# Sums over keys in an attention kernel: four TensorE transposes per block replaced by VectorE's 32x32 transposes and one small TensorE transpose

## The chip, the cores and the metric

The kernel runs on one core of a Trainium2 chip. A core has five engines with instruction streams of their own, each executed in order: TensorE (PE in the profile, its weight loads PEld), VectorE (DVE), ScalarE (ACT), GpSimd (POOL) and SyncE (SP, which here only issues DMAs). They share SBUF (128 partitions) and synchronise by semaphores. TensorE writes its results to PSUM, whose banks hold 128 partitions of 512 float32 numbers. The metric is the device time of one execution in microseconds (us); lower is better.

## The reference, cut to what matters

The whole computation is one encoder layer over 2048 tokens: an input projection, a gated linear attention with 4 heads (group A), a latent attention with 4 heads (group B), an output projection and a layer norm. The change touches only the softmax of group B:

```python
def attend(blk):
    qn, qr = blk
    s = (jnp.einsum('bqhd,bkhd->bhqk', qn, k_nope, preferred_element_type=jnp.float32)
         + jnp.einsum('bqhr,bkr->bhqk', qr, k_r, preferred_element_type=jnp.float32))
    p = jax.nn.softmax(s, axis=-1)
    return jnp.einsum('bhqk,bkhv->bqhv', p.astype(v.dtype), v)
```

For each head and query, the exponentials of the scores less their maximum are summed over all 2048 keys, and the weighted values are divided by that sum. The kernel leaves the division to the output projection: it stores the reciprocal of the sum for every head and query, and multiplies by it there.

## The kernel before, in words

After the input projection and group A, the function `attention` works through 16 blocks. A block is one head and 512 queries (`QB`); four heads for one range of queries follow each other. Within a block the keys lie on the partitions: `scores(i, j)` computes the scores of a pair of key tiles, 2 x 128 keys against 512 queries, as 10 matmuls of 128x512 into one of two PSUM tiles `pS`, and there are 8 such steps j in a block. Float32 products are made of three matmuls of rounded parts (`mm3`), so each product has a high and a low operand (`ph` and `pl` for the exponentials).

What follows for each step: ScalarE copies the scores to an SBUF tile `s` (`copy`, L1571). VectorE folds them from PSUM into a running maximum `rm` of 128 partitions x 512 queries (`smax`, L1584; L1581 for step 0). After step 7 PE transposes `rm` (`tmax`, L1590), VectorE takes the maximum over the keys that are left (`rmax`, L1595), and PE spreads it over the partitions again into `mb` (`bmax`, L1602). VectorE subtracts it (`sub`, L1608), ScalarE takes the exponential (`exp`, L1612) and the high part (`phi`, L358), GpSimd the low part (`plo`, L364), and PE multiplies with the values into the PSUM tile `o` (`pv`, 6 matmuls a step, L412 to L414). A `pS` tile can be written again when `copy` and `smax` have read it.

Sums over keys: VectorE adds the exponentials of steps 0, 1, 2 and 5 into a PSUM tile `ap` (`acc`, L1635), GpSimd those of the other four into an SBUF tile of 128 x 2 x 512 named `acc` (L1638, L1640). `tot` (L1658, L1659) adds the two, so that `acc[:, 0]` holds, for each partition, a sum over 16 keys for each of the 512 queries. The 128 partitions are still to be added. `tsum` (L1671) transposes this 128x512 by four PE transposes of 128x128 into the PSUM tile `sx`, with the data as weights and the identity as the moving operand. `rcp` adds along the row on VectorE (L1677, a reduction of 128x512 to 128x4) and takes the reciprocal (L1678). `keep` (L1683) sends the 128x4 result to `r_s` in HBM from ScalarE's DMA queue, in pieces of 4 bytes, since neighbouring queries lie on neighbouring partitions.

The result in `o` is split into `ofh` (ScalarE, `oh`) and `ofl` (VectorE, `ol`), which both read the one PSUM bank of `o`, and multiplied with the value weights (`y`, `yc`). `sx`, the transposed maxima and `y` use the same bank in turn (`pX`, tag x). The output projection (`OutProj.load`) reads `r_s` back, broadcast over the partitions.

The order of the work is written out by hand: `PLACE` gives each piece a place in steps from the start of its own step (or, for the pieces once a block, from its step 7), `put` collects them, and they are traced in order of place; `in_order` ties each engine's instructions to this order. In these units a block is 8 steps. `tot` at 7 + 11.2 stands at 2.2 of the block two later, `tsum` at 3.04, `rcp` at 4.55, `keep` at 5.21. Around them stand, in that same later block: `smax` of step 1 at 2.21, the fourth `sub` of the block before at 2.37, scores of step 3 at 3 and of step 4 at 4, and the first `pv` of the block before at 4.35.

The last two blocks differ: their sums are stored as rows, by a PE transpose (`turn`, L1689) and a DMA from SyncE's queue (`rows`, L1696), and part of their work is placed among the output projection.

Of the kernel before, what the change touches and what calls it, by code (L numbers as in the profile page):

```python
# [9 lines left out]
F32 = mybir.dt.float32  # L10
# [3 lines left out]
ALU = mybir.AluOpType  # L14
AX = mybir.AxisListType
# [3 lines left out]
P = 128  # L19
# [10 lines left out]
QB = 512  # L30
# [62 lines left out]
    rmax=1.27,  # L93
    bmax=1.48,
    tot=11.2,
    tsum=12.04,
    rcp=13.55,
    keep=14.21,
    oh=12.34,
    ol=12.99,  # L100
    y=16.55,
    yc=16.9,
# [244 lines left out]
class K:  # L347
# [1190 lines left out]
    def attention(self):  # L1538
        tc, nc = self.tc, self.nc
        mm = nc.tensor.matmul  # L1540
        V, G, Ac = nc.vector, nc.gpsimd, nc.scalar
        NP = NKT // 2
        with ExitStack() as ctx:
# [3 lines left out]
            bs = ctx.enter_context(tc.tile_pool(name="bs", bufs=2, reuse_waits="tile"))  # L1547
            bank = lambda n, bufs=1: ctx.enter_context(tc.tile_pool(name=n, bufs=bufs, space=PSUM, reuse_waits="tile"))
            pM, pO, pX, pA, pS = bank("pM"), bank("pO"), bank("pX"), bank("pA"), bank("pS", 2)
            blocks = [(h, b) for b in range(NQB) for h in range(H)]  # L1550
            nb = len(blocks)
            stt = [dict(s=[None] * NP) for _ in blocks]
# [108 lines left out]
            def close(i, shape, name, other):  # L1661


                p, tag = other if i == nb - 1 else (pX, "x")
                return p.tile(shape, F32, tag=tag, name=name)

            def tsum(i):
                d = stt[i]
                d["x"] = close(i, [P, 4, P], f"sx{i}", (pA, "ap"))
                for e in range(4):  # L1670
                    nc.tensor.transpose(d["x"][:, e], d["as"][:, 0, e * P:(e + 1) * P], self.ident)  # L1671

            def rcp(i):

                d = stt[i]
                rc = bs.tile([P, 4], F32, tag="rc", name=f"rc{i}")
                V.tensor_reduce(rc, d["x"], AX.X, ALU.add)  # L1677
                V.reciprocal(rc, rc)  # L1678
                d["rc"] = rc

            def keep(i):
                h, b = blocks[i]
                Ac.dma_start(self.r_s[b][:, h].rearrange("o (e p) -> p (o e)", p=P), stt[i]["rc"])  # L1683

            def turn(i):

# [48 lines left out]
            def put(place, fn, *a):  # L1735
                todo.append((place, len(todo), fn, a))
# [5 lines left out]
            put(0.5, nc.sync.dma_start, wv, self.ins["wv"])  # L1742
            put(8.6, wv_hi)
            put(9.9, self.lo, wv_l, wv, wv_h, "pool")
            own = (("tot", tot), ("tsum", tsum), ("rcp", rcp), ("keep", keep), ("oh", oh), ("ol", ol), ("y", y), ("yc", yc))
            own_late = tuple(e for e in own if e[1] is not keep)
            for i in range(nb):
                for j in range(NP):
                    t = NP * i + j
# [80 lines left out]
            for c in range(4, NCH):  # L1830
                with fixed():
                    split(c + 2)
                    load(c + 4)
                    if 4 < c < NCH - 1:
                        op.load_res(rest[c + 1])
                    op.product(rest[c])
                    op.finish(rest[c])
                with self.after(*last.values()), fixed():
                    for f in {4: (tot, oh, ol), 5: (tsum, rcp), 7: (turn, y, rows, yc)}.get(c, ()):
                        f(nb - 1)  # L1840
                    if c == 6:
                        turn(nb - 2)
                        rows(nb - 2)
# [216 lines left out]
```

## Time and profile before

| | us |
|---|---|
| median of 3 runs | 1270.41 |
| lowest and highest | 1268.89, 1271.71 |
| the profiled execution | 1270.53 |
| its span in the profile | 1268.4 |
| first group of L1671 in the trace, block 0 | 643.6 |
| L1671 of block 13 | 1048.4 |
| last group of L1671, block 15 | 1147.9 |

The span runs from the first to the last recorded instruction; all times of views count from its start. A row of a group gives line, engine, operation, the tiles written and read, shapes and count, then busy time, mean duration in ns, and the engine's idle time before these instructions with what ended most of it. A row of the timeline gives start and duration in us, engine, line, operation, tiles and count; a bracket at its end gives idle time before it and what released it. Neighbouring instructions of a group stand in one row. PE's matmuls are pipelined, so their records overlap. "PEclk" is the clock granted to TensorE, in tenths of full speed in the page and as a fraction in the table of windows.

### The profile page before, as it was taken

The page shows a single profiled execution, that of the slowest core. Times are in us where ns is not written, and L with a number is a line of the kernel's source. Part 1 is how long each engine was busy: PE and PEld are TensorE (multiplying, and loading weights), DVE is VectorE, ACT ScalarE, POOL GpSimd, SP SyncE. Part 2 cuts the span into 40 slices and gives each one's busy share as a digit, 9 for nine tenths or more (in the row PEclk, how much of TensorE's full clock was granted, in tenths as well). Part 3 has the DMA queues.
Part 4 walks back from the last instruction along what each step waited for, and adds up shares of the span by engine and source line. Part 5 has one row for each costly group of instructions (what it writes and reads, how often), then busy time and mean ns, then how long its engine had stood idle before and what let it go on. Part 6 is the DMA issues. An engine that isn't in the chain of part 4 may idle for free.

```text
span 1268.4 us, 19649 instructions
## 1 busy us (share of the span) xinstructions
PE 1247.2 (98%) x6950; PEld 1100.2 (87%) x6950; DVE 893.5 (70%) x1610; ACT 727.9 (57%) x1177; POOL 718.6 (57%) x443
## 2 busy tenths in 40 slices
PE   8999999999999999989999999999999999999997
PEld 7999999999899999988788888888888888887886
DVE  6635555553665545564888888888888888389997
ACT  7544343454665444444888888888888888411110
POOL 0132323223265554430798888889999999935541
PEclk9999999999999999999999999999999999999999
DMA  8224555565857766747211111202133120376662
GB/s 297 76 82 124 136 144 137 144 134 159 274 173 211 210 187 204 211 133 199 76 32 53 40 45 42 59 9 59 58 92 92 42 42 26 122 231 195 208 191 100
DMA packets 188546, 160.10 MB, mean 126 GB/s; under 512 B 97206, under 2 KB 139838, under 8 KB 188448
## 3 DMA queue, kind: packets, MB, share of 16 engines
q1 hardware_dynamic: 180384, 156.72, 43.2%
q0 software_dynamic: 672, 2.10, 0.4%
q8 instruction: 55, 0.90, 0.3%
q10 hardware_dynamic: 7392, 0.03, 0.3%
q14 instruction: 43, 0.35, 0.1%
HBM read 102.79 MB, written 56.00 MB: 125 GB/s over the span
## 4 chain that ended last, share of the span: by engine, by line
PE 87%; issue 3%; DMA 3%; POOL 2%; DVE 2%; ACT 2%; SPq 1%; DVEq 0%; POOLq 0%; ACTq 0%
PE pz L1244 7%; PE ipm L1315 5%; PE o L412 5%; PE o L413 5%; PE o L414 4%; PE pS L1562 4%; PE pS L1563 4%; PE pS L1564 4%; PE pS L1565 4%; PE pS L1566 4%; PE ipa L412 4%; PE ipa L414 4%; PE ipa L413 4%; PE ipg L414 2%; PE ipg L413 2%
## 5 line engine op out<-in xcount | busy, mean ns | idle before, releaser
L364 POOL TENSOR_TENSOR pl<-s,ph 128x1024 fp32r<-128x1024 f32 x128 | 306.7, 2415 | 51.5 <-ACT ph L358 48.0
L1584 DVE TENSOR_TENSOR rm<-pS,rm 128x512 f32<-128x512 f32 x210 | 144.8, 690 | 36.3 <-ACT s L1571 30.7
L1571 ACT ACTIVATE s<-pS 128x1024 f32<-128x1024 f32 x128 | 131.2, 1025 | 61.3 <-PE pS L1566 51.7
L1608 DVE TENSOR_TENSOR s<-s,mb 128x1024 f32<-128x1024 f32 x128 | 151.2, 1213 | 8.9 <-PE mb L1602 8.2
L358 ACT ACTIVATE ph<-s 128x1024 fp32r<-128x1024 f32 x128 | 135.0, 1056 | 17.2 <-PE o L414 16.5
L1612 ACT ACTIVATE s<-s 128x1024 f32<-128x1024 f32 x128 | 131.4, 1049 | 9.4 <-DVE s L1608 9.3
L412 PE MATMUL ipa<-wah,xah 128*128 128x384 f32 (+1 forms) x384 | 128.8, 335 | 5.5 <-ACT wah L358 5.5
L413 PE MATMUL ipa<-wal,xah 128*128 128x384 f32 (+1 forms) x384 | 124.5, 324 | 0.0
L414 PE MATMUL ipa<-wah,xal 128*128 128x384 f32 (+1 forms) x384 | 124.5, 324 | 0.0
L1079 POOL TENSOR_TENSOR Sb<-Sb,Us 64x512 f32<-64x512 f32 x15 | 19.9, 1324 | 169.7 <-DVE Us L1071 160.6
L1562 PE MATMUL pS<-qh,ckvT_h 128*128 128x512 f32 x256 | 102.6, 401 | 0.8 <-DVE rm L1584 0.4
L412 PE MATMUL o<-ph,vh 128*128 128x512 f32 x256 | 101.1, 395 | 0.0
L1563 PE MATMUL pS<-ql,ckvT_h 128*128 128x512 f32 x256 | 100.0, 391 | 0.0
L1564 PE MATMUL pS<-qh,ckvT_l 128*128 128x512 f32 x256 | 99.9, 390 | 0.0
L1565 PE MATMUL pS<-rh,krs 128*128 128x512 f32 x256 | 99.9, 390 | 0.0
L1566 PE MATMUL pS<-rl,krs 128*128 128x512 f32 x256 | 99.8, 390 | 0.0
L414 PE MATMUL o<-ph,vl 128*128 128x512 f32 x256 | 99.8, 390 | 0.0
L413 PE MATMUL o<-pl,vh 128*128 128x512 f32 x256 | 99.7, 389 | 0.0
L1635 DVE TENSOR_TENSOR ap<-ap,s 128x512 f32<-128x512 f32 x120 | 83.0, 692 | 2.7 <-ACT s L1612 0.7
L412 PEld LDWEIGHTS ipa<-wah,xah 128*128 128x128 f32 x384 | 73.1, 190 | 8.4 <-ACT wah L358 5.5
L364 POOL TENSOR_TENSOR ol<-of,oh 128x512 fp32r<-128x512 f32 x32 | 43.0, 1344 | 64.3 <-ACT oh L358 64.3
L413 PEld LDWEIGHTS ipa<-wal,xah 128*128 128x128 f32 x384 | 73.2, 191 | 0.8 <-DVE wal L364 0.2
(302 smaller groups left out, 3427.3 us busy)
## 6 DMA issues: line engine op xcount, KB each, us to landing
xcf<-xT_dram SPq DMA_DIRECT2D x16, 512.0 KB, 5.4
xr<-x_dram SPq DMA_DIRECT2D x16, 512.0 KB, 6.3
out_dram<-rr SPq DMA_DIRECT2D x32, 256.0 KB, 2.1
xaf<-xT_dram SPq DMA_DIRECT2D x14, 512.0 KB, 4.2
oib<-oi_s SPq DMA_DIRECT2D x16, 256.0 KB, 3.7
qdb<-qd_s SPq DMA_DIRECT2D x16, 256.0 KB, 3.5
SU<-su_s SPq DMA_DIRECT2D x16, 256.0 KB, 3.9
ub<-u_s SPq DMA_DIRECT2D x16, 256.0 KB, 3.9
```

The costliest lines, as they stand in the source:

```text
L358: return nc.scalar.activation(dst, src, AF.Copy).ins
L364: return e.tensor_tensor(dst, src, hi.bitcast(F32), ALU.subtract).ins
L412: mm(out, ah, bh, start=start, stop=False)
L413: mm(out, ah, bl, start=False, stop=False)
L414: mm(out, al, bh, start=False, stop=stop)
L1562: mm(ps[:, e], kh, qh, start=True, stop=False)
L1563: mm(ps[:, e], kh, ql, start=False, stop=False)
L1564: mm(ps[:, e], kl, qh, start=False, stop=False)
L1565: mm(ps[:, e], kr, rh, start=False, stop=False)
L1566: mm(ps[:, e], kr, rl, start=False, stop=True)
L1584: V.tensor_tensor(d["rm"], src[:, e], d["rm"], ALU.max)
L1608: V.tensor_tensor(s, s, d["mb"][:, None, :].to_broadcast([P, 2, QB]), ALU.subtract)
```

## The change

For blocks 0 to 13 the sums over the 128 partitions are made in another way. A new piece `tpart` follows `tot` on VectorE: it transposes each 32x32 square of the 128x512 in `acc[:, 0]` into `acc[:, 1]` (which `tot` has read and nobody needs any more), so that 32 keys of a query now lie in one row, and adds each run of 32: a tile `s16` of 128x16. For partition 32k + r, column b of it holds the sum over the 32 keys of group k for query 32b + r. `tsum` transposes `s16` by one PE transpose into 16 rows of 128. `rcp` adds the four groups k with a strided reduction, 16x128 to 16x32, and takes the reciprocal of 16x32. `keep` stores these as 16 rows of 32 numbers, 128 bytes each, from the same queue. `tsum` moves from 12.04 to 12.44, `tpart` stands at 11.25. Blocks 14 and 15 are as before, but for the name of a tag.

```diff
     tot=11.2,
-    tsum=12.04,
+    tpart=11.25,
+    tsum=12.44,
     rcp=13.55,
...
+            def tpart(i):
+                d = stt[i]
+                V.transpose(d["as"][:, 1], d["as"][:, 0])
+                d["s16"] = bs.tile([P, QB // 32], F32, tag="s16", name=f"s16_{i}")
+                V.tensor_reduce(d["s16"], d["as"][:, 1].rearrange("p (b k) -> p b k", k=32), AX.X, ALU.add)
+
             def tsum(i):
                 d = stt[i]
+                if i < nb - 2:
+                    d["x"] = pX.tile([P, 4, P], F32, tag="x", name=f"sx{i}")[0:QB // 32, 0]
+                    nc.tensor.transpose(d["x"], d["s16"], self.ident)
+                    return
                 d["x"] = close(i, [P, 4, P], f"sx{i}", (pA, "ap"))
                 for e in range(4):
                     nc.tensor.transpose(d["x"][:, e], d["as"][:, 0, e * P:(e + 1) * P], self.ident)
...
             def rcp(i):
 
                 d = stt[i]
-                rc = bs.tile([P, 4], F32, tag="rc", name=f"rc{i}")
+                if i < nb - 2:
+                    rc = d["rc"] = bs.tile([QB // 32, 32], F32, tag="rc", name=f"rc{i}")
+                    V.tensor_reduce(rc, d["x"].rearrange("b (k q) -> b q k", k=4), AX.X, ALU.add)
+                    V.reciprocal(rc, rc)
+                    return
+                rc = bs.tile([P, 4], F32, tag="rc4", name=f"rc{i}")
                 V.tensor_reduce(rc, d["x"], AX.X, ALU.add)
                 V.reciprocal(rc, rc)
                 d["rc"] = rc
 
             def keep(i):
                 h, b = blocks[i]
-                Ac.dma_start(self.r_s[b][:, h].rearrange("o (e p) -> p (o e)", p=P), stt[i]["rc"])
+                Ac.dma_start(self.r_s[b][:, h].rearrange("o (e q) -> (o e) q", q=32), stt[i]["rc"])
...
-            own = (("tot", tot), ("tsum", tsum), ("rcp", rcp), ("keep", keep), ("oh", oh), ("ol", ol), ("y", y), ("yc", yc))
-            own_late = tuple(e for e in own if e[1] is not keep)
+            own = (("tot", tot), ("tpart", tpart), ("tsum", tsum), ("rcp", rcp), ("keep", keep), ("oh", oh), ("ol", ol), ("y", y), ("yc", yc))
+            own_late = tuple(e for e in own if e[1] not in (keep, tpart))
```

## The prediction

> **What bounds the kernel now.** First the page: the engines' busy times, the granted clock and the chain that ended last.
>
> ```profile
> span 1268.4 us, 19649 instructions
> ...
> PE 1247.2 (98%) x6950; PEld 1100.2 (87%) x6950; DVE 893.5 (70%) x1610; ACT 727.9 (57%) x1177; POOL 718.6 (57%) x443
> ...
> PEclk9999999999999999999999999999999999999999
> ...
> PE 87%; issue 3%; DMA 3%; POOL 2%; DVE 2%; ACT 2%; SPq 1%; DVEq 0%; POOLq 0%; ACTq 0%
> ```
>
> TensorE carries 87% of the chain and its clock is never held back. Whole-span shares mix stages, so next the busy times of single attention blocks (from one group of the transposes L1671 to the next) and TensorE's waits from 612 to 1076 us.
>
> ```profile
> core 0: us, PE busy (x) PEld busy (x) DVE busy (x) ACT busy (x) POOL busy (x), PEclk, DMA share, GB/s
> 706.04:737.17 31.13, 31.13 (x145) 25.77 (x143) 27.01 (x37) 25.31 (x27) 26.23 (x12) 1.00 0.18 43
> ...
> 986.16:1017.28 31.12, 31.12 (x145) 25.77 (x144) 26.99 (x37) 26.34 (x29) 30.61 (x15) 1.00 0.17 43
> 1017.28:1048.40 31.12, 31.12 (x144) 25.77 (x143) 27.00 (x37) 26.34 (x29) 30.96 (x16) 1.00 0.18 35
> 1048.40:1076.06 27.66, 27.66 (x128) 22.61 (x127) 23.38 (x32) 22.24 (x24) 27.58 (x13) 1.00 0.05 11
> ```
>
> ```profile
> PE pS L1562 <- ACT s L1612: 0.4, 1, 0.4
> ```
>
> A block takes 31.12 us and TensorE fills it; in 464 us it waits once, 0.4 us. Each TensorE nanosecond taken from a block shortens the kernel, as long as nothing else becomes late. VectorE is the engine to fear, at 27.0 of 31.1 us, and GpSimd (POOL) in the last blocks, at 30.6, 30.96 and then 27.58 of 27.66 us.
>
> **What the removed transposes cost.** The duration of a matmul record is no price here, since records overlap; the price is the distance between starts. Below, in time order on PE, one group of L1671, then the only single small transpose in the trace (L1689, which comes after a wait), and the group's piece of the chain.
>
> ```profile
> 705.81 0.39 PE L1566 MATMUL pS<-rl,krs 128*128 128x512 f32 x1
> 706.04 0.60 PE L1671 MATMUL sx<-ident,acc 128*128 128x128 f32 x4
> 706.39 0.48 PE L1562 MATMUL pS<-qh,ckvT_h 128*128 128x512 f32 x1
> 706.71 0.40 PE L1563 MATMUL pS<-ql,ckvT_h 128*128 128x512 f32 x1
> ```
>
> ```profile
> 1160.38 0.27 PE L1689 MATMUL rt<-ident,rc 128*4 128x128 f32 x1 [0.93 <-DVE rc L1677]
> 1160.41 0.48 PE L412 MATMUL po<-woh,oh 128*128 128x512 f32 x1
> 1160.73 0.39 PE L413 MATMUL po<-wol,oh 128*128 128x512 f32 x1
> ```
>
> ```profile
> 1048.56 0.44 PE sx L1671 x4
> ```
>
> An ordinary step is 0.23 us (705.81 to 706.04). Four transposes hold the next matmul back by 0.35 us (706.04 to 706.39), and the step after it is 0.32 instead of 0.23: 0.44 in all, which is the chain's piece. One small transpose holds it back by 0.03, with the same 0.32 behind it: 0.12. So one in place of four saves 0.32 us a block. The new one has 16 columns as weights, where L1689 has 4; 128 columns stream through in both, so I take L1689's price. Bounds: 0.26 saved, if the new one holds the matmul back by its share of the group, a quarter of 0.35, and the slower step of 0.09 stays; 0.41, if it holds it back by 0.03 and the slower step goes too. Times 14 blocks: 4.5 us, 3.6 to 5.7.
>
> In the Trainium skill, "TensorE: Matmul & The Clock Gate", section "Part 4: PE-mode transpose", a transpose inside a kernel lasts about 275 ns; the duration of 0.27 us above agrees, but the start distances do not bear it out as a cost in a filled pipe. By that figure three fewer in 14 blocks would be an estimated 11.6 us.
>
> PE's order does not change. In steps of a block (eight to a block), the transposes stood at 3.04 of the block two later and now stand at 3.44, and between the scores at 3 and at 4 nothing else is issued on PE.
>
> **What VectorE gets.** Rows for the prices:
>
> ```profile
> L1491 DVE STREAM_TRANSPOSE oT<-og 128x512 f32<-128x512 f32 x16 | 11.4, 712 | 0.5
> L1474 DVE TENSOR_REDUCE Ob<-og 128x4 f32<-128x512 f32 x16 | 11.1, 693 | 9.3 <-ACT og L1469 9.3
> L1677 DVE TENSOR_REDUCE rc<-sx 128x4 f32<-128x512 f32 x16 | 10.9, 679 | 0.0
> L1678 DVE RECIPROCAL rc<-rc 128x4 f32<-128x4 f32 x16 | 2.8, 178 | 0.5
> L1509 DVE TENSOR_TENSOR rope<-pqr,sin 128x128 f32<-128x128 f32 x32 | 7.6, 280 | 0.0
> ```
>
> And VectorE's order in one block, after the maxima of step 1:
>
> ```profile
> 700.13 1.41 DVE L1584 TENSOR_TENSOR rm<-pS,rm 128x512 f32<-128x512 f32 x2
> 701.45 1.21 DVE L1608 TENSOR_TENSOR s<-s,mb 128x1024 f32<-128x1024 f32 x1
> ...
> 706.16 0.68 DVE L364 TENSOR_TENSOR ofl<-o,ofh 128x512 fp32r<-128x512 f32 x1
> 707.36 1.42 DVE L1584 TENSOR_TENSOR rm<-pS,rm 128x512 f32<-128x512 f32 x2 [0.52 <-ACT s L1571]
> ...
> 709.29 0.68 DVE L1677 TENSOR_REDUCE rc<-sx 128x4 f32<-128x512 f32 x1
> 710.00 0.18 DVE L1678 RECIPROCAL rc<-rc 128x4 f32<-128x4 f32 x1
> 710.10 1.41 DVE L1635 TENSOR_TENSOR ap<-ap,s 128x512 f32<-128x512 f32 x2
> ...
> 712.54 2.93 DVE L1584 TENSOR_TENSOR rm<-pS,rm 128x512 f32<-128x512 f32 x4
> ```
>
> The new pair comes at 2.25, behind the maxima of step 1 (2.21) and ahead of a subtraction (2.37): at 701.45. Transpose 0.71 (the same shape, L1491) and reduction 0.69 (same elements, also from SBUF, L1474; 16 sums instead of 4). An instruction that needs the one before starts 0.03 after its end (709.97 to 710.00), an independent one 0.09 ahead of it (701.54 to 701.45): 0.71 + 0.03 + 0.69 - 0.09 = 1.34 us. Bounds 1.31 (the reduction at 0.68, less rounding) to 1.45 (no overlap).
>
> In the place of 709.29 the reduction of 128x512 becomes one of 16x128. No row shows that shape: 0.18 below (L1678), 0.68 above (L1677); I take 0.28, the row with as many elements per partition (L1509). The reciprocal of 16x32 lies between 0.18 (L1678) and 0.68; I take 0.23, near the row with the same operation. The two were 0.81 from 709.29 to 710.10 and become 0.28 + 0.03 + 0.23 - 0.08 = 0.46: 0.35 less.
>
> The Trainium skill, "VectorE: DVE Perf Modes", section "First, the fixed hardware budget", gives the reciprocal a repeat of eight; 28 more elements would by that add an estimated 0.23 us to L1678's, 0.41 in all, and the maxima of step 4 below would have 0.17 us to spare. No row here shows it.
>
> Net, VectorE gains 1.34 - 0.35 = 1.0 us a block, to 28.0 of 30.8. The question is who waits while it is late. Three matmuls of PE need a PSUM bank that VectorE has read:
>
> ```profile
> 708.80 0.39 PE L412 MATMUL o<-ph,vh 128*128 128x512 f32 x1
> ...
> 710.16 0.39 PE L1562 MATMUL pS<-qh,ckvT_h 128*128 128x512 f32 x1
> ...
> 715.14 0.39 PE L1562 MATMUL pS<-qh,ckvT_h 128*128 128x512 f32 x1
> ```
>
> What such a wait costs is seen once, at the start of attention:
>
> ```profile
> 609.21 1.41 DVE L1584 TENSOR_TENSOR rm<-pS,rm 128x512 f32<-128x512 f32 x2
> ...
> 610.76 0.47 PE L1562 MATMUL pS<-qh,ckvT_h 128*128 128x512 f32 x1 [0.43 <-DVE rm L1584]
> ```
>
> VectorE ends at 610.62, PE starts at 610.76: 0.14 us. The three, with PE 0.32 earlier than before:
>
> - The first P*V matmul of the next block needs the o bank, which ofl reads. VectorE has no gap from 701.45 on, so ofl is 1.34 late: it ends at 708.18, plus 0.14 is 708.32; PE comes at 708.48. Spare: 0.16.
> - Scores of step 5 need the maxima of step 3. These had 0.52 us of idle and 0.09 of overlap ahead of them, so they are 0.73 late and end at 709.51; 709.65 against 709.84. Spare: 0.19.
> - Scores of step 6 need the maxima of step 4: late by 0.73 - 0.35 = 0.38, ending at 712.54 + 1.41 + 0.38 = 714.33; 714.47 against 714.82. Spare: 0.35.
>
> All hold, the first two barely. A matmul's weights are normally loaded a step ahead, and a wait that spoils this alone lengthens the next step by 0.09 (0.32 instead of 0.23, as above): at two places 0 to 0.18 us a block. I take 0.04, 0.6 us over 14. The rest of the lateness ends at 718.73, where this row has 0.80 us of idle:
>
> ```profile
> 718.73 1.42 DVE L1584 TENSOR_TENSOR rm<-pS,rm 128x512 f32<-128x512 f32 x2 [0.80 <-ACT s L1571]
> ```
>
> GpSimd's 30.96 us in the block before 1048 exceeds the new 30.8 by 0.16, and 27.58 exceeds 27.34 by 0.24 after it: 0 to 0.4 us in all, as its products run ahead of PE; I take 0.2.
>
> **The wait, the DMA, the banks.** PE's transpose now waits for the sums: ready at 701.45 + 1.43 = 702.88 and wanted at 706.04, so nothing is queued behind it. The rows go out through ScalarE's queue as before, 14 times:
>
> ```profile
> L1683 ACTq DMA_DIRECT2D r_s<-rc x14: 366/366/387, 648.0 to 1052.6; - x14
> ...
> L1696 SPq DMA_DIRECT2D r_s<-rt x2: 287/287/287, 1179.5 to 1188.8; - x2
> ```
>
> 16 rows of 128 bytes are nearer to the second than to the 512 pieces of 4 bytes of the first: 0 to 0.08 us less on ScalarE. The instruction waits for the reciprocal some 0.4 us longer, with a copy of scores running in ScalarE meanwhile: nothing. The half of acc that takes the transposed copy is free, as VectorE itself read it last.
>
> **The sum.** 4.5 - 0.6 - 0.2 = 3.7 us. The profiled execution took 1270.53 us (span 1268.4, 2.1 around it), 0.1 above the median of 1270.41: 1266.8 from the one, 1266.7 from the other. Own range, with one bound at a time: 5.7 - 0.8 = 4.9 saved (1265.5) to the restarts at their full 0.18, 4.5 - 2.5 - 0.2 = 1.8 saved (1268.6); with no restart and the most saved it reaches 1264.7.
>
> **Rivals.**
> - VectorE's lateness eats the saving: at the o bank a delay of 1.34 + 0.16 + 0.32 = 1.82 us would take back all 0.32. For it speak spare times of 0.16 and 0.19, smaller than one restart; against it, that both prices have rows of their own shape. Two restarts (0.18) and 0.14 of real stall a block leave nothing: 1270.4.
> - Slower: the two small VectorE instructions are not small. At their upper ends, 0.68 each, 0.81 becomes 1.31, the maxima of step 4 are 0.73 + 0.50 = 1.23 late, and scores of step 6 stall by 1.23 - 0.73 = 0.50 a block (their spare is 0.73 at no lateness). That is 0.50 - 0.32 = 0.18 lost, 2.5 us over 14: 1272.9; with a restart of 0.09 added, 1274.2. It begins to cost at 0.73 of lateness, takes all back at 1.05. For it: neither shape has a row. Against: 128 elements at 280 ns.
> - Each transpose holds PE for its recorded 0.27 us: 3 x 0.27 x 14 = 11.3 saved, 1259.1. The distance of 0.35 for four speaks against it. This is the page's figure named above.
> - The change does not reach the path: GpSimd bounds the late blocks. Only three windows are near it, so this stays inside the forecast's range.
>
> **Chances.** Forecast 0.68, saving eaten 0.17, slower 0.13, long transposes 0.02. A change of 0.2%, 2.5 us, is what a measurement here can tell. Of the forecast's 0.68, 0.04 lies above 1267.9: faster 0.64 + 0.02 = 0.66, same 0.17 + 0.04 = 0.21, slower 0.13. The range 1265.3 to 1270.6 holds the forecast but for its lowest end (0.03) and most of the second case; it leaves out the slower one, the long transposes and these ends, 0.2 in all.
>
> **What would show it.** Right: blocks of 30.8 to 30.9 us between transposes; sx x1 with 0.03 to the next start; a transpose of 0.71 and a reduction of 0.69; the small pair under 0.5 us together; no idle on PE from 644 to 1048. Wrong: PE waits at the o matmul L412 or at L1562 on rm or ofl; a small pair near 1 us; a block at 31.1 us.

## The result and the profile after

| | us |
|---|---|
| kernel before, median of 6 runs beside the changed one | 1270.38 |
| changed kernel, median of 6 runs | 1265.06 |
| its lowest and highest | 1264.78, 1266.36 |
| ratio to the kernel before (95% interval) | 0.9958 (0.9948 to 0.9968) |
| its profiled execution, and its span | 1265.56, 1263.8 |

The kernel is faster by 5.3 us; the forecast was 3.7, and 1265.06 lies 0.24 us below the range. The page of the changed kernel:

```profile
span 1263.8 us, 19578 instructions
...
PE 1242.2 (98%) x6908; PEld 1093.4 (87%) x6908; DVE 905.9 (72%) x1638; ACT 730.8 (58%) x1177; POOL 719.2 (57%) x443
...
PEclk9999999999999999999999999999999999999999
...
PE 87%; DMA 3%; issue 3%; DVE 2%; POOL 2%; ACT 1%; SPq 1%; DVEq 0%; POOLq 0%; ACTq 0%
```

TensorE is the bound as before. VectorE has 12.4 us more to do over 14 blocks, 0.9 a block. Single blocks, from one transpose to the next, in the table of windows:

```profile
767.66:798.47 30.81, 30.81 (x142) 25.38 (x140) 27.95 (x39) 25.53 (x27) 26.22 (x12) 1.00 0.14 43
...
983.36:1014.15 30.79, 30.79 (x142) 25.39 (x140) 27.94 (x39) 26.34 (x29) 30.29 (x15) 1.00 0.14 40
1014.15:1044.98 30.83, 30.83 (x141) 25.37 (x140) 27.97 (x39) 26.46 (x29) 30.67 (x16) 1.00 0.13 38
1044.98:1072.35 27.37, 27.37 (x126) 22.27 (x125) 24.38 (x33) 22.41 (x24) 27.29 (x13) 1.00 0.03 10
```

A block takes 30.8 us instead of 31.12, also the late ones in which GpSimd (the fifth busy time) was feared. The timeline of PE at the transpose, and its piece in the chain:

```profile
705.78 0.39 PE L1567 MATMUL pS<-rl,krs 128*128 128x512 f32 x1
706.01 0.27 PE L1678 MATMUL sx<-ident,s 128*16 128x128 f32 x1
706.04 0.48 PE L1563 MATMUL pS<-qh,ckvT_h 128*128 128x512 f32 x1
706.35 0.40 PE L1564 MATMUL pS<-ql,ckvT_h 128*128 128x512 f32 x1
```

```profile
706.17 0.11 PE sx L1678
```

The one transpose of 16 columns holds the next matmul back by 0.03 us and the step after it is 0.31, just as the transpose of 4 columns did: 0.11 us on the chain where 0.44 stood.

The groups of VectorE's new instructions, and its timeline in the block of 706:

```profile
L1670 DVE STREAM_TRANSPOSE acc<-acc 128x512 f32<-128x512 f32 x14 | 9.8, 702 | 0.0
L1672 DVE TENSOR_REDUCE s<-acc 128x16 f32<-128x512 f32 x14 | 9.6, 686 | 0.5
L1690 DVE RECIPROCAL rc<-rc 16x32 f32<-16x32 f32 x14 | 4.8, 341 | 0.5
L1689 DVE TENSOR_REDUCE rc<-sx 16x32 f32<-16x128 f32 x14 | 3.8, 270 | 0.0
```

```profile
701.42 0.70 DVE L1670 STREAM_TRANSPOSE acc<-acc 128x512 f32<-128x512 f32 x1
702.16 0.69 DVE L1672 TENSOR_REDUCE s<-acc 128x16 f32<-128x512 f32 x1
702.76 1.21 DVE L1609 TENSOR_TENSOR s<-s,mb 128x1024 f32<-128x1024 f32 x1
703.89 1.41 DVE L1585 TENSOR_TENSOR rm<-pS,rm 128x512 f32<-128x512 f32 x2
...
707.47 0.68 DVE L365 TENSOR_TENSOR ofl<-o,ofh 128x512 fp32r<-128x512 f32 x1
708.07 1.41 DVE L1585 TENSOR_TENSOR rm<-pS,rm 128x512 f32<-128x512 f32 x2
...
710.00 0.27 DVE L1689 TENSOR_REDUCE rc<-sx 16x32 f32<-16x128 f32 x1
710.30 0.34 DVE L1690 RECIPROCAL rc<-rc 16x32 f32<-16x32 f32 x1
710.57 1.40 DVE L1636 TENSOR_TENSOR ap<-ap,s 128x512 f32<-128x512 f32 x2
...
713.00 2.93 DVE L1585 TENSOR_TENSOR rm<-pS,rm 128x512 f32<-128x512 f32 x4
```

From 701.42 to 702.76 the pair takes 1.34 us, and no bracket of idle time stands before the maxima of step 3 (708.07) any more. The three matmuls of PE that need a bank which VectorE has read, as listed in the prediction:

```profile
708.43 0.40 PE L413 MATMUL o<-ph,vh 128*128 128x512 f32 x1
...
709.82 0.39 PE L1563 MATMUL pS<-qh,ckvT_h 128*128 128x512 f32 x1
...
714.81 0.39 PE L1563 MATMUL pS<-qh,ckvT_h 128*128 128x512 f32 x1
```

ofl ends at 708.15, 0.28 ahead of the first; the maxima of step 3 at 709.48, 0.34 ahead of the second; those of step 4 at 713.00 + 1.41 = 714.41, 0.40 ahead of the third. Less the 0.14 us of a wait that the prediction took, 0.14, 0.20 and 0.26 us are left. For the first, the experiments below show a shorter wait, 0.05 us, so that its matmul has 0.23 us. But the weights of that matmul are loaded ahead of it, and their load, too, comes only after ofl:

```profile
708.21 0.19 PEld L413 LDWEIGHTS o<-ph,vh 128*128 128x128 f32 x1
```

It starts 0.06 us after the end of ofl, so the load has no time to spare.

Where the 4.97 us between the two profiled executions lie: the first scores of attention started 0.60 us later (582.68 before, 583.28 after), in a part that the change doesn't touch; the blocks gave 4.33 (the transposes of the maxima of block 15 stand at 1064.17 and 1060.44, 3.73 earlier, and 0.60 more from the later start); the tail gave 0.9 more (the last matmul starts at 1260.09 and 1255.45), and the time outside the span fell from 2.1 to 1.8. The tail's 0.9 us is one wait: the single transpose rt, quoted in the prediction with 0.93 us of idle before it, has none in the timeline of the changed kernel:

```profile
1155.70 0.27 PE L1705 MATMUL rt<-ident,rc 128*4 128x128 f32 x1
```

### The profile page after: what moved, and what is told of

Read it like the earlier page. It is cut to its first block, busy times and chain, and to the rows that moved or that the text cites. A ratio compares the mean times of both kernels' runs of the same rounds, so it can differ in the third digit from the quotient of the medians.

```text
span 1263.8 us, 19578 instructions
## 1 busy us (share of the span) xinstructions
PE 1242.2 (98%) x6908; PEld 1093.4 (87%) x6908; DVE 905.9 (72%) x1638; ACT 730.8 (58%) x1177; POOL 719.2 (57%) x443
## 4 chain that ended last, share of the span: by engine, by line
PE 87%; DMA 3%; issue 3%; DVE 2%; POOL 2%; ACT 1%; SPq 1%; DVEq 0%; POOLq 0%; ACTq 0%
PE pz L1245 7%; PE ipm L1316 5%; PE o L413 5%; PE o L414 5%; PE o L415 5%; PE pS L1563 5%; PE pS L1565 4%; PE pS L1564 4%; PE pS L1567 4%; PE pS L1566 4%; PE ipa L413 4%; PE ipa L415 4%; PE ipa L414 4%; PE ipg L415 2%; PE ipg L413 2%
```

## The experiments

Block times below are the 13 distances between neighbouring groups of the transposes of the maxima on PE, from block 1 to block 14; the two unaltered kernels had 31.12 to 31.16 before and 30.80 to 30.84 after.

### The same two kernels again

The changed kernel, unaltered (r1_after; a third time as r3_after), and the kernel before (r2_before).

> The changed kernel once more, for what is noise in its gain. If the whole gain sits in the attention blocks (14 x 0.31 us) and the 0.9 us that the first profile gained after them (TensorE's wait before the first rt transpose, gone) is chance of DMA landings, the time is again 4 to 6 us below the kernel before, the blocks are 30.8 us apart again, and the wait before rt may come back. If the tail's gain belongs to the change, that wait is near 0 again here and near 0.9 us in the repeated kernel before.

> The kernel before once more: ratio 1.000 within 0.1%. Blocks 31.12 us apart. TensorE's wait before the first rt transpose was 0.93 us in the first profile: anything from 0 to 1.5 us if it is chance, 0.8 to 1.0 if it belongs to this kernel.

> The changed kernel a third time, as the measure for the two below, on the same chip: 4 to 5.5 us below the kernel before; blocks of 30.8 to 30.86 us.

r1_after: 1266.55 us (1264.75 to 1267.63), ratio 0.9963 (0.9951 to 0.9976); blocks of 30.82 to 30.85. r3_after: 1265.85 (1263.75 to 1268.86), ratio 0.9964 (0.9953 to 0.9974); blocks of 30.79 to 30.84. The kernels before beside them had 1271.02 and 1269.99: gains of 4.5 and 4.1 us. r2_before: ratio 1.0005 (0.9996 to 1.0013), blocks of 31.09 to 31.12. The rt transpose in the timelines, of r2_before and then of r1_after:

```profile
1160.90 0.27 PE L1689 MATMUL rt<-ident,rc 128*4 128x128 f32 x1 [0.47 <-DVE rc L1677]
```

```profile
1156.95 0.27 PE L1705 MATMUL rt<-ident,rc 128*4 128x128 f32 x1
```

The wait is half as long in the repeat of the kernel before. Of the variants below, those of the kernel before show 0.65 us (e2_dve) and no bracket (e7_keep16). Those of the changed kernel that keep this transpose show 0.60 us (e4_dve_b) and no bracket (e1_pe3, e3_dve_a, e6_rcp), as the changed kernel itself in its three profiles. So the wait can come with either kernel and be absent with either. But it stands in three of four profiles of the one kind and in one of seven of the other; whether some of it goes with the change stays open.

The blocks alone, from the transposes of the maxima of block 0 to those of block 15, take 460.49 and 460.17 us in the two profiles of the kernel before and 456.16, 456.57 and 456.21 in the three of the changed kernel. By which two are compared, the blocks gain 3.6 to 4.3 us, and the first pair is the upper end.

### PE's part undone

```diff
                 if i < nb - 2:
-                    d["x"] = pX.tile([P, 4, P], F32, tag="x", name=f"sx{i}")[0:QB // 32, 0]
+                    x = pX.tile([P, 4, P], F32, tag="x", name=f"sx{i}")
+                    for e in range(1, 4):
+                        nc.tensor.transpose(x[:, e], d["as"][:, 0, e * P:(e + 1) * P], self.ident)
+                    d["x"] = x[0:QB // 32, 0]
                     nc.tensor.transpose(d["x"], d["s16"], self.ident)
```

> The changed kernel with three more PE transposes of 128x128 in each of blocks 0 to 13, whose results nobody reads: PE's part undone, VectorE's part kept. If the gain is PE's start distances, 3 x 0.105 us a block come back: blocks of 31.12 to 31.14 us, 4.4 us above the changed kernel, within 0.8 us of the kernel before. If the gain comes from the smaller store or from the tail, at most 1 us comes back. If each transpose costs its recorded 0.27 us, 11 us come back.

1270.17 us, ratio 0.9997 (0.9988 to 1.0006): the whole gain is gone, though VectorE's new work and the new store are still there. Blocks of 31.08 to 31.16. The timeline of PE in e1_pe3:

```profile
708.19 0.49 PE L1679 MATMUL sx<-ident,acc 128*128 128x128 f32 x3
708.52 0.27 PE L1681 MATMUL sx<-ident,s 128*16 128x128 f32 x1
708.54 0.48 PE L1563 MATMUL pS<-qh,ckvT_h 128*128 128x512 f32 x1
```

Three transposes fill 0.33 us (708.19 to 708.52), 0.11 each, though each is recorded with 0.27. The price is the start distance. The figure of about 275 ns for a transpose (of bf16) inside a kernel that the Trainium skill gives ("TensorE: Matmul & The Clock Gate", section "Part 4: PE-mode transpose") agrees with the recorded duration and not with this price; by it, e1_pe3 would have ended 11.6 us above the changed kernel, and it ended 5.1 above its first median and 3.6 above r1_after's.

### VectorE's part alone

The kernel before with the function `tpart` of the change added at 11.25, its sums unused, and `tsum`, at its new place 12.44, still with four transposes.

> The kernel before with VectorE's new pair (32x32 transpose and reduction) added and its result not used; the four PE transposes and the store as before: VectorE's part alone. If its lateness is absorbed, as its spare times say (with PE 0.32 us later than in the changed kernel, 0.3 to 0.5 us at every edge): blocks of 31.12 us, 0 to 0.5 us above the kernel before. If the added 1.34 us of VectorE stall PE, 0.1 us a block or more: 1.5 us or more above it.

1270.59 us, ratio 0.9998 (0.9989 to 1.0007), blocks of 31.12 to 31.16. One block of e2_dve in the table of windows:

```profile
707.86:738.99 31.13, 31.13 (x144) 25.75 (x143) 28.23 (x39) 25.65 (x27) 26.19 (x12) 1.00 0.17 43
```

VectorE (28.23, before 27.0) is 1.2 us busier and the block as long as before: where PE is 0.32 us later, the lateness is hidden.

### One small transpose more on VectorE

```diff
                 V.transpose(d["as"][:, 1], d["as"][:, 0])
+                V.transpose(d["as"][:, 1, 0:P], d["as"][:, 0, 0:P])
```

> The changed kernel with one more VectorE transpose, of 128x128 (about 0.25 us), between the new transpose and the reduction in blocks 0 to 13: VectorE's lateness raised a little, PE's work unchanged. My theory (spare times of 0.16 and 0.19 us at the o bank and before the scores of step 5): the spare is used up, PE's matmul there starts about 0.1 us late and the next step is longer by 0.09: blocks of 30.9 to 31.0 us instead of 30.8, 1 to 3 us more. Rival: the spare is far larger than worked out, and nothing changes (30.8).

1270.06 us, ratio 0.9992 (0.9982 to 1.0001), blocks of 31.06 to 31.14. The changed kernel's ratios were 0.9958 to 0.9964, so 0.28 to 0.34% or 3.6 to 4.3 us more, above what was expected: one small transpose on VectorE takes nearly all of the gain. Its price was expected to be 0.25 us. VectorE's timeline shows 0.34: from the first transpose to the subtraction pass 1.68 us (702.98 to 704.66), where the changed kernel has 1.34.

```profile
702.98 0.70 DVE L1670 STREAM_TRANSPOSE acc<-acc 128x512 f32<-128x512 f32 x1
703.71 0.31 DVE L1671 STREAM_TRANSPOSE acc<-acc 128x128 f32<-128x128 f32 x1
...
704.66 1.21 DVE L1609 TENSOR_TENSOR s<-s,mb 128x1024 f32<-128x1024 f32 x1
...
709.38 0.68 DVE L365 TENSOR_TENSOR ofl<-o,ofh 128x512 fp32r<-128x512 f32 x1
```

The waits of PE's weight loads in e3_dve_a (total, times, longest), and one of them in the timelines of weight loads and of matmuls:

```profile
PEld o L413 <- DVE ofl L365: 5.0, 13, 0.4
```

```profile
710.11 0.19 PEld L413 LDWEIGHTS o<-ph,vh 128*128 128x128 f32 x1 [0.39 <-DVE ofl L365]
```

```profile
709.76 0.39 PE L1567 MATMUL pS<-rl,krs 128*128 128x512 f32 x1
710.11 0.50 PE L413 MATMUL o<-ph,vh 128*128 128x512 f32 x1
710.45 0.39 PE L414 MATMUL o<-pl,vh 128*128 128x512 f32 x1
```

The o matmul comes 0.35 us after its neighbour instead of 0.23, and the step behind it takes 0.34: 0.12 late and 0.11 for the restart. The place is the one expected, but the numbers behind it were not. ofl ends at 709.38 + 0.68 = 710.06, and the matmul and its weight load both start at 710.11, 0.05 later; it is 0.05 in all 13 such places of e3_dve_a, and in all 13 of e4_dve_b below. So a wait costs 0.05 us here and not 0.14, the matmul of the changed kernel has 0.28 - 0.05 = 0.23 us to spare, and 0.34 - 0.23 = 0.11 is its lateness. That 0.25 - 0.14 gives 0.11 as well is luck. In the first of the blocks the matmul is hardly late, a step of 0.26 us (647.60 to 647.86), and the step behind it is 0.34 all the same (to 648.20).

The block lost 0.3 us, and these two steps make 0.23. Set beside the blocks of the changed kernel step by step, the rest is no second wait. It lies in the dozen steps behind the late matmul and in some at the scores of step 6, each longer by less than 0.01 us on average. Why they are longer stays open.

### 0.7 us more at two places

e4_dve_b does the new 128x512 transpose twice; e6_rcp has one more such transpose behind the reciprocal.

```diff
                 V.transpose(d["as"][:, 1], d["as"][:, 0])
+                V.transpose(d["as"][:, 1], d["as"][:, 0])
```

```diff
                     V.reciprocal(rc, rc)
+                    V.transpose(d["as"][:, 1], d["as"][:, 0])
                     return
```

> The changed kernel with the 128x512 transpose done twice (0.7 us more of VectorE at the same place). Theory: 0.7 - 0.16 = 0.5 us of stall and 0.1 for the restart: blocks of 31.3 to 31.5 us, 7 to 10 us more than the changed kernel, so slower than the kernel before; PE's waits on ofl or rm show in the profile. Rival: VectorE has idle time enough (3 us a block) to take it: 30.8.

> The changed kernel with one more 128x512 VectorE transpose (0.7 us) behind the reciprocal, where the prediction's slower rival puts its price; its result is not used. Theory: the maxima of step 4 have 0.27 us to spare before the scores of step 6 in the changed kernel's profile, so 0.7 - 0.27 = 0.4 us of stall and 0.1 for the restart: blocks of 31.2 to 31.4 us, 6 to 8 us more. Rival: the later idle time takes it and blocks stay at 30.8.

e4_dve_b: 1275.39 us, ratio 1.0036 (1.0022 to 1.0049), blocks of 31.46 to 31.54. e6_rcp: 1272.29, ratio 1.0007 (0.9998 to 1.0017), blocks of 31.18 to 31.26. Windows and waits of PE in e4_dve_b:

```profile
706.75:738.26 31.51, 31.29 (x142) 25.22 (x140) 28.64 (x41) 25.54 (x27) 26.25 (x12) 1.00 0.17 42
```

```profile
PE o L413 <- DVE ofl L365: 3.1, 13, 0.3
```

```profile
705.38 1.41 DVE L1585 TENSOR_TENSOR rm<-pS,rm 128x512 f32<-128x512 f32 x2
...
706.75 0.27 PE L1679 MATMUL sx<-ident,s 128*16 128x128 f32 x1
706.93 0.47 PE L1563 MATMUL pS<-qh,ckvT_h 128*128 128x512 f32 x1
```

This is a fourth edge, which the prediction did not list: scores of step 4 need the maxima of step 2. Those end at 705.38 + 1.41 = 706.79, and PE starts at 706.93, 0.14 later, with 0.18 us behind its transpose instead of 0.03: 0.15 us late. In the changed kernel they end at 703.89 + 1.41 = 705.30 for a start at 706.04, which leaves 0.60 us, and the second transpose puts VectorE 0.75 us behind (from the first transpose at 702.16 to the subtraction at 704.25 pass 2.09 us instead of 1.34). The o matmul then comes 0.38 us late (709.09 to 709.70 in place of 0.23) and the step behind it is 0.10 longer (to 710.03); together 0.63 of the 0.70 us that the block lost.

And in e6_rcp a block, and PE's timeline before the scores of step 6:

```profile
707.76:739.02 31.26, 31.13 (x142) 25.30 (x141) 28.46 (x40) 25.53 (x27) 26.29 (x12) 1.00 0.16 43
```

```profile
716.35 0.39 PE L415 MATMUL o<-ph,vl 128*128 128x512 f32 x1
716.87 0.47 PE L1563 MATMUL pS<-qh,ckvT_h 128*128 128x512 f32 x1
717.18 0.40 PE L1564 MATMUL pS<-ql,ckvT_h 128*128 128x512 f32 x1
```

A step of 0.52 in place of 0.23, then 0.31: 0.37 us at the third edge. The sizes are near what was expected, e4_dve_b's block a little above it and e6_rcp's at its lower end. VectorE has 2.8 us of idle time left in a block, and still 0.7 us at these places stops PE.

### The store alone

The kernel before with its store in 128 pieces of 16 bytes. The reciprocals land at other places of `r_s`, so the output of this kernel is another one; it serves for the time alone.

```diff
-                Ac.dma_start(self.r_s[b][:, h].rearrange("o (e p) -> p (o e)", p=P), stt[i]["rc"])
+                Ac.dma_start(self.r_s[b][:, h].rearrange("o (p e) -> p (o e)", p=P), stt[i]["rc"])
```

> The kernel before with its 14 stores in pieces of 16 bytes (128 of them) instead of 4 (512); the reciprocals land at other places, so the output is another one. The store's part alone. Theory: hidden, 0 +- 0.8 us against the kernel before, blocks of 31.12 us. If the small pieces held up ScalarE's queue or the loads of the tail, 0.9 us or more would go, and PE's wait before the first rt with it.

1270.96 us, ratio 1.0001 (0.9992 to 1.0010); blocks of 31.12 and 31.13. The smaller number of pieces is hidden. The changed kernel goes further, to 16 pieces; that step is in e1_pe3, where none of the gain is left. In the changed kernel the store's group reads

```profile
L1699 ACTq DMA_DIRECT2D r_s<-rc x14: 308/308/353, 649.0 to 1049.6; - x14
```

with a median of 1.3 us to landing, where the 4-byte pieces took 9.5: much for the DMA, nothing for the kernel.

### Versions with block 14, and with the pair split

e8_b14 does block 14 in the new way too, without its rt transpose and its store as rows. e9_split moves the reduction behind the maxima of step 3 besides, with the transpose, the small pair and the store after it. e10_split14 does so for blocks 0 to 13 and leaves block 14 at e8_b14's places.

```diff
-    tsum=12.44,
-    rcp=13.55,
-    keep=14.21,
+    tred=13.3,
+    tsum=14.05,
+    rcp=15.25,
+    keep=15.75,
+    tsum14=12.44,
+    rcp14=13.55,
+    keep14=14.21,
...
             def tpart(i):
                 d = stt[i]
                 V.transpose(d["as"][:, 1], d["as"][:, 0])
+
+            def tred(i):
+                d = stt[i]
                 d["s16"] = bs.tile([P, QB // 32], F32, tag="s16", name=f"s16_{i}")
...
-                if i < nb - 2:
+                if i < nb - 1:
...
-            own_late = tuple(e for e in own if e[1] not in (keep, tpart))
+            own_late = (("tot", tot), ("tpart", tpart), ("tpart", tred), ("tsum14", tsum), ("rcp14", rcp), ("keep14", keep),
+                        ("oh", oh), ("ol", ol), ("y", y), ("yc", yc))
...
-                    if c == 6:
-                        turn(nb - 2)
-                        rows(nb - 2)
```

> The changed kernel with block 14 done in the new way too: its four transposes, its rt transpose, ScalarE's copy of it and SyncE's store go, and its row goes out by ScalarE's queue. Theory: 0.32 us less on PE, 0.1 for the rt transpose, and PE's wait before it (0, 0.14 and 0.9 us in four profiles) cannot come back or moves to the next product: 0.3 to 1 us less, at the edge of what can be measured. Rival: VectorE's added 1.3 us falls into the tail, where VectorE's chain of residuals ends late: 0 to 1 us more.

> As e8_b14, and VectorE's pair is split: the transpose stays behind the maxima of step 1, the reduction moves behind those of step 3 (place 13.3), and the PE transpose (14.05), the small pair (15.25) and the store (15.75) move behind it. VectorE is then 0.7 instead of 1.3 us late at the o bank and hardly late before step 5. Theory: the last 0.02 to 0.05 us of stall a block go, blocks of 30.77 to 30.80 us, 0.3 to 0.7 us less than e8_b14. Rival: the later transposes or the store meet another wait (the shared bank, ScalarE's queue) and blocks grow to 30.9 us or more.

> As e9_split for blocks 0 to 13 (blocks were 30.79 us, with no stall left), and block 14 at the places that it has in e8_b14, since in e9_split TensorE waited 2.1 us there for the late reduction. Theory: blocks of 30.79 us, no wait at block 14's transpose, 0.3 to 0.5 us below e8_b14's level of 0.9959 of the kernel before: 0.995 to 0.996. If the late places of e9_split cost elsewhere too, 0.997 or more.

e8_b14: 1264.57 us, ratio 0.9959 (0.9946 to 0.9971), blocks of 30.82 to 30.86; the further gain that was expected is too small to be told apart from the changed kernel. e9_split: 1266.51, ratio 0.9975 (0.9966 to 0.9984): its blocks are 30.78 to 30.82, but PE waits in the tail for block 14's reduction, which now stands late in VectorE's order:

```profile
1076.37 0.27 PE L1682 MATMUL sx<-ident,s 128*16 128x128 f32 x1 [2.10 <-DVE s L1676]
```

e10_split14: 1264.13 us, ratio 0.9955 (0.9941 to 0.9968), a first block of 30.82 and twelve of 30.79, and no such wait. The split takes the last 0.03 us from a block, as expected. The weights of the o matmul are then loaded 0.64 us after the end of ofl (709.32, and 708.00 + 0.68) and not right behind it. It has the lowest median of all, but its interval overlaps those of the changed kernel (0.9958, 0.9963 and 0.9964), so faster than the changed kernel is not shown.

## Why the prediction was right and where it was wrong

- PE is the bound and a start distance is the price: right. e1_pe3 takes the gain back with VectorE's new work and the new store in place, and e2_dve and e7_keep16 show nothing for those two. PE has no wait from 644 to 1048 in the changed kernel, as was said.
- The size of PE's saving: 0.32 us a block worked out. Where least stalls (e10_split14, 30.79), it is 0.33 against the first profile's 31.12 and 0.30 against the shortest blocks of r2_before, 31.09.
- VectorE's pair, 1.34 us: exact. The small reduction, 0.28: 0.27. The reciprocal was taken as 0.23 and is 0.34; its bounds (0.18 to 0.68) held it. With it the small pair takes 0.57 us (710.00 to 710.57) where 0.46 was worked out, and under 0.5 was named as a sign of being right: that sign did not come. It cost no time, as the third edge kept 0.26 us. The Trainium skill's repeat of eight for a reciprocal ("VectorE: DVE Perf Modes", section "First, the fixed hardware budget") gave an estimated 0.41: nearer than the row of a smaller one.
- The three edges: spare of 0.16, 0.19 and 0.35 worked out; 0.14, 0.20 and 0.26 by the profile, if a wait is 0.14 us. The lateness was read rightly, but the price of the wait came from another place. Before scores it is 0.14 (e4_dve_b), at the o matmul 0.05: 0.23 us to spare for the matmul and none for its weight load. e3_dve_a and e4_dve_b stop PE at the first edge, e6_rcp at the third. No run stopped it at the second, before scores of step 5. The fourth, before scores of step 4, was not on the list; with 0.60 us it holds in the changed kernel.
- The restarts were taken as 0.04 us a block, 0.6 us in all. No restart shows in the changed kernel: in its three profiles no step of the 13 blocks is longer than 0.24 us, but for those right behind transposes. Its blocks are 0.03 longer than e10_split14's, 0.4 us in all, in steps longer by 0.01 us or less. The size was near by luck. GpSimd's 0.2 us did not come: with 30.67 of 30.83 us busy it still runs ahead of PE.
- So the blocks gave 4.3 us in the first pair of profiles where the sum had 3.7. The two losses, 0.8 together, were over-estimated by 0.4. The other 0.2 is within what the blocks' gain differs between pairs of profiles (3.6 to 4.3).
- The step that failed is the sum, 4.5 - 0.6 - 0.2 = 3.7, taken for the whole kernel, and the range built on it. It put everything outside the blocks at nothing, without a reason, and it is there that 1.0 of the 5.3 us lie. The profiles show 0.6 us of it. The wait before rt in the tail was 0.93 us in the profile that the sum was made against, 0.47 in its repeat, and is gone in the changed kernel's, which gave 0.9. The time outside the span gave 0.3, and the later start of attention took 0.6 back. The rest is scatter between runs: the medians differ by 5.3 us and the profiled executions by 4.97. Why the wait before rt comes and goes stays open.
- The low end of 1265.3 was built from prices alone, and a part of the forecast's own range (down to 1264.7) was cut off. The table of times showed a spread: the lowest of three runs of the kernel before lay 1.5 us under their median. Chance has its part in the miss: the two repeats of the changed kernel, 1266.55 and 1265.85, lie inside the range.
- The slower rival, small instructions of 0.68 each, did not come, but its arithmetic holds: e6_rcp, with 0.7 us at that place, has blocks 0.1 us longer than the kernel before's. The rival of the saving eaten was put at a delay of 1.82 us at the o bank. e3_dve_a, with 1.34 + 0.34 = 1.68, is nearly that case, with blocks of 31.06 to 31.14.

## What to carry to other kernels

When the pipe of TensorE is full, price a matmul or transpose by the distance between starts, not by its record. Before giving work to an engine with idle time, list the points at which the bound engine needs its results and subtract the lateness from each; here VectorE's 2.9 us of idle time in a block of the changed kernel leave 0.20 us before scores of step 5, 0.23 at the o matmul and none at its weight load. Take the price of a wait from the same kind of place; it was 0.05 us at one and 0.14 at another. And a range needs the spread of the runs added to the bounds of the prices.

## What the runs showed of the hardware

A VectorE reciprocal of 32 numbers a partition (on 16 partitions) takes 0.34 us, one of 4 (on 128) takes 0.18: 28 more cost 0.16, about 6 ns each, while a reduction over 128 numbers a partition needs 0.27 in all. The time from VectorE's end to PE's start is not one number: 0.05 us at the o matmul, where the weight load waits as well (26 places in e3_dve_a and e4_dve_b), and 0.14 before the scores of step 4 in e4_dve_b. And a wait at a weight load lengthens the next step by about 0.1 us, even where the matmul is hardly late: in e3_dve_a a matmul 0.03 us late was followed by a step of 0.34 instead of 0.23, as were those 0.12 late.
